# Modulation rows summed by halves, with additions made by accumulating DMAs, in a one-core hybrid decoder block

## The chip, the cores and the metric

The kernel runs on one core of a Trainium2 chip. The core has five engines that each work through their own queue in order: TensorE (PE, with its weight loads shown apart as PEld), VectorE (DVE), ScalarE (ACT), GpSimd (POOL) and SyncE (SP). Transfers are issued from the queues of SP, ACT and POOL and run on 16 shared DMA engines. The metric is the device time of one execution in microseconds (us); lower is better. A profiled execution's span runs from its first to its last instruction on the engines, and its own time is a little longer.

## What is computed

The reference is one layer of a decoder trunk on x (1 x 512 x 1024, float32), conditioned by a vector c of 1024 numbers. The layer has two sub-layers, and each is wrapped in normalisation and in shift, scale and gate rows that come from c:

```python
mod = jax.nn.silu(c) @ mod_w + mod_b
shift1, scale1, gate1, shift2, scale2, gate2 = [m[:, None, :] for m in jnp.split(mod, N_MOD, axis=-1)]

h = rms_norm(x, g_pre_mix) * (1 + scale1) + shift1
(sc_b, sc_c, sc_x, q, k, v, z, xbc, dt_raw,
 gl_a, gl_b, gl_c) = split_columns(h @ w_in)
y_a = short_conv_mixer(sc_b, sc_c, sc_x, sc_conv_w) @ w_sc_out
y_b = stick_breaking_attention(q, k, v) @ w_sb_out
y_c = mamba2_mixer(z, xbc, dt_raw, ...) @ w_ssm_out
merged = (jax.nn.sigmoid(gl_a) * y_a + jax.nn.sigmoid(gl_b) * y_b
          + jax.nn.sigmoid(gl_c) * y_c)
x = x + gate1 * rms_norm(merged @ w_o, g_post_mix)

h2 = rms_norm(x, g_pre_ffn) * (1 + scale2) + shift2
gt, up = jnp.split(h2 @ w_ffn_in, 2, axis=-1)
x = x + gate2 * rms_norm((silu(gt) * up) @ w_ffn_out, g_post_ffn)
```

`mod_w` is 1024 x 6144: six parts of 1024 columns, one each for shift1, scale1, gate1, shift2, scale2 and gate2. What the change touches is the sum over the 1024 rows of `mod_w` for parts 2 to 5, the addition of `mod_b`, and the sum of the three gated branches in `merged`.

## The kernel before

Every large product is made exact to nearly float32 by splitting each operand into a rounded high part and a low rest: `split` (L146) copies the high part on ACT and subtracts it on DVE, and `mm3` (L150) multiplies high by high, high by low and low by high. Activations are kept with channels on the 128 partitions and the 512 tokens along the columns, so a typical matmul is 128 x 128 by 128 x 512, and a product over 1024 channels is 24 matmuls.

**Weights.** SP loads weights in chunks of up to 1 MB into a ring of three buffers (`raw_tile`, L74). `chunks` (L163) is the list of them in order of use; `load_chunk` (L175) issues the next. A weight chunk is split into pieces of 128 x 1024; `piece` (L212) hands out the next piece and sees to it that two further ones are already split (`LOOK` = 3); four buffers hold the split pieces. Chunks of kind "mod" are raw rows of `mod_w`; they stay unsplit, and `mod_chunk` (L221) hands them out.

**The start** (L316 to L399) has an order written out by hand. Here `start_mod` (L250) forms the sums for shift1 and scale1, 128 columns of each at a time, and `start_col` (L260) turns them into columns. The result tile of a step, `out_` (L256), lies in the small pool `sm`.

**Behind the start** the order on each engine is set by a planner. It takes the program's order as priority, estimates when each instruction's inputs will be there, and lets an engine that would stand idle take a later instruction that is ready. Attention's softplus steps are marked as high priority. What it decides is then fixed: on the chip each engine runs its queue in that order.

**The mixers.** `attention` (L560), `ssd` (L673) and `mods_in_turn` (L894) are generators that run beside the projections: each call of `pump` (L835) lets every one of them emit its next step. `gate` (L881) projects one 128-channel tile of a branch gate (24 matmuls into a tile `pgt`), pumps once, and takes the sigmoid. Six gates are formed first (L888); then a loop over `mp` = 0 to 3 (L936) forms six further gates and handles two tiles m of 128 merged channels. For each, three branch products `pb` are multiplied by their gate tile on DVE (L954); the second and third are added to the running sum on DVE (L956); the sum `acc` is split into `mh[m]` and `ml[m]` (L958 to L960). Tiles of 128 x 512 that live for a short time come from one pool of 41 (`t2`, L67).

**The modulation rows** of parts 2, 3 and 4 (gate1, shift2, scale2) are made in `mods_in_turn` during those gates, by quarters of 256 columns. For a quarter, `sums` (L896) loads 256 numbers of `mod_b` from POOL's queue (L903). It then forms the sum of eight products with `mod_acc` (L228): partition p of the chunk holds rows 8p to 8p+7 of `mod_w`, each is multiplied by silu(c) for that row and added, all on DVE. The bias row is added into partition 0 on DVE (L906) and the result is split (L908). One or two pumps later, `row` (L911) sums over the partitions with two matmuls by a matrix of ones. This leaves the row on all partitions, and DVE or ACT takes it out of PSUM into `G1`, `SH` or `SC` (L917 to L921). Part 5 (gate2) is made in the same way during the first half of the last product (L1088).

**The output projection** (L1012 to L1027) takes two blocks of 128 tokens at a time. For each of the first five of eight row steps k it multiplies `mh[k]`, `ml[k]` by a piece of `w_o`, 12 matmuls for both blocks; the last three steps are done block by block, so that the chain behind the first block (`x1_chain`, L975) starts early. Ahead of it POOL issues four loads of x (L967 to L968) into the buffer that the third branch used. The feed-forward part (from L1030) follows.

Of the kernel before, what the change touches and what calls it, by code (L numbers as in the profile page):

```python
# [13 lines left out]
P = 128  # L14
# [18 lines left out]
def hybrid_block(ctx: ExitStack, tc, x, c, mod_w, mod_b, g_pre_mix, g_post_mix, g_pre_ffn,  # L33
# [193 lines left out]

    def mod_acc(acc, mw):  # L228

        vec.tensor_scalar(acc, mw[:, 0], sc8[:, 0:1], None, op0=ALU.mult)  # L230
        for r in range(1, KD):
            vec.scalar_tensor_tensor(acc, mw[:, r], sc8[:, r:r + 1], acc, op0=ALU.mult,  # L232
                                     op1=ALU.add)


# [216 lines left out]

    def w_mod(part, q4):
        n0 = part * D + q4 * 256
        chunks.append(("mod", [[(0, KD, mod_w[:, n0:n0 + 256])]], 256, 0))
# [5 lines left out]
    mods = [(p_, q4) for p_ in (2, 3, 4) for q4 in range(4)]  # L461
    w_cols(w_in, C_XBC + 384, P)
# [20 lines left out]
    for hf in range(2):  # L483
        for k0 in range(0, MF, 4):
            w_rows(w_ffn_out, k0, min(4, MF - k0), half(hf), 512)
            if hf == 0 and k0 // 4 < 4:
                w_mod(5, k0 // 4)
    n_pieces = sum(ch[3] * len(ch[1]) for ch in chunks)
# [405 lines left out]
    def mods_in_turn(steps, rest):  # L894

        def sums(part, q4):  # L896
            dsts, gain, plus = rows_of[part]
            n0 = part * D + q4 * 256
            if gain is not None and q4 % 2 == 0:
                nc.gpsimd.dma_start(dsts[q4 // 2],  # L900
                                    gain[0, q4 * 256:q4 * 256 + 512].partition_broadcast(P))
            brow = sm.tile([1, 256], F32, tag="brow", name="brow", bufs=2)
            nc.gpsimd.dma_start(brow, mod_b[n0:n0 + 256].unsqueeze(0))  # L903
            acc = sm.tile([P, 256], F32, tag="macc", name="macc2")
            mod_acc(acc, mod_chunk())
            vec.tensor_tensor(acc[0:1, :], acc[0:1, :], brow, ALU.add)  # L906
            am = sm.tile([P, 2, 256], FR, tag="mah", name="mah", bufs=1)
            split(am[:, 0, :], am[:, 1, :], acc)  # L908
            return am

        def row(part, q4, am):  # L911
            dsts, gain, plus = rows_of[part]
            dst = dsts[q4 // 2][:, (q4 % 2) * 256:(q4 % 2) * 256 + 256]
            pm = bank("pmr")
            pe.matmul(pm[:, 0:256], onesr, am[:, 0, :], start=True, stop=False)
            pe.matmul(pm[:, 0:256], onesr, am[:, 1, :], start=False, stop=True)
            if gain is None:  # L917
                act.copy(dst, pm[:, 0:256])
            else:
                vec.scalar_tensor_tensor(dst, pm[:, 0:256], plus, dst, op0=ALU.add,  # L920
                                         op1=ALU.mult)  # L921
        last = None
        for n, st_ in enumerate(steps):
            if last is not None:
                row(*last)
            last = st_ + (sums(*st_),)
            yield
            if rest and n % 2:
                yield
# [3 lines left out]

    mh, ml = [], []
    sides.append(mods_in_turn(mods, True))
    for mp in range(4):  # L936
# [6 lines left out]
        for j in range(2):  # L943
# [3 lines left out]
            for b, (k0, nk, bh, bl) in enumerate(((0, 2, yah, yal), (2, 2, ybh, ybl),  # L947
# [7 lines left out]
                if b:  # L955
                    vec.tensor_tensor(gt, gt, acc, ALU.add)  # L956
# [55 lines left out]
    for tp2 in range(2):  # L1012
# [63 lines left out]
    for hf in range(2):  # L1076
# [5 lines left out]
        for i in range(NPF - LATE):  # L1082
# [3 lines left out]
            if hf == 0:  # L1086
                if i == 0:
                    sides.append(mods_in_turn([(5, q4) for q4 in range(4)], False))  # L1088
                pump()
# [59 lines left out]
```

## Time and profile before

| | us |
|---|---|
| median of 3 runs | 808.54 |
| lowest and highest | 807.54, 809.47 |
| profiled execution, its own time | 807.41 |
| span of the profiled execution | 805.7 |
| mean granted TensorE clock in it | 0.997 of full speed |

The profile names instructions by line and by tile: L232 is line 232, `macc` the modulation sum, `wraw` a chunk of weights, `whi` and `wlo` a split piece. An arrow reads "written from". "Idle before <- releaser" tells how long an engine stood idle ahead of an instruction, and what ended that. On a page or in a view, busy time of PE counts matmuls that overlap, since each lasts longer than the distance to the next one.

### The profile page before, as it was taken

How to read it: one execution, taken by the hardware profiler on the slowest of the kernel's cores; microseconds unless marked ns; L12 is line 12 of the kernel's file. 1: busy time of each engine (PE TensorE's matmuls, PEld its weight loads, DVE VectorE, ACT ScalarE, POOL GpSimd, SP SyncE). 2: the span in 40 equal slices, each digit the busy share in tenths (PEclk: the TensorE clock that was granted, in tenths of full speed). 3: DMA queues.
4: the chain of work that ended last, by engine and by line, in shares of the span. 5: the costliest groups of instructions: out<-in, count | busy, mean ns of one | idle time of the engine just before them, and what ended most of it. 6: DMA issues, size and time to landing. Idle time of an engine off the chain costs nothing.

```text
span 805.7 us, 9651 instructions
## 1 busy us (share of the span) xinstructions
PE 775.2 (96%) x3677; PEld 634.2 (79%) x3677; DVE 495.5 (62%) x783; ACT 373.2 (46%) x625; POOL 122.5 (15%) x169
## 2 busy tenths in 40 slices
PE   3899999999899999999999999999999999999997
PEld 2679887767578888888878988888888888888886
DVE  5999968568967968748498544334344357423214
ACT  5566544565667445463465534434334433213112
POOL 4453412345421000000033000000000000000000
PEclk9999999999999999999999999999999999999999
DMA  9981441120534566452754322322333345532102
GB/s 281 297 258 58 130 131 53 53 85 31 184 121 154 187 201 206 129 173 101 262 169 145 102 84 78 103 81 79 102 105 104 105 148 195 170 115 96 35 1 105
DMA packets 96959, 105.07 MB, mean 130 GB/s; under 512 B 3276, under 2 KB 86272, under 8 KB 96912
## 3 DMA queue, kind: packets, MB, share of 16 engines
q1 hardware_dynamic: 94320, 99.62, 38.6%
q0 software_dynamic: 1824, 3.75, 1.6%
q10 hardware_dynamic: 768, 1.07, 0.4%
q8 instruction: 29, 0.48, 0.2%
q14 instruction: 18, 0.15, 0.1%
HBM read 102.33 MB, written 2.10 MB: 130 GB/s over the span
## 4 chain that ended last, share of the span: by engine, by line
PE 83%; DVE 11%; DMA 2%; issue 2%; ACT 1%; POOL 1%; DVEq 0%; POOLq 0%
PE pgt L151 5%; PE pgt L153 5%; PE pgt L152 5%; PE pfg L152 5%; PE pfu L152 5%; PE pfu L151 5%; PE pfg L151 5%; PE pfu L153 4%; PE pfg L153 4%; PE pfo L152 4%; PE pfo L153 4%; PE pfo L151 4%; DVE smacc L254 2%; PE pbr L151 2%; PE pbr L152 2%; PE pbr L153 2%
## 5 line engine op out<-in xcount | busy, mean ns | idle before, releaser
L147 ACT CAST whi<-wraw 128x1024 fp32r<-128x1024 f32 (+1 forms) x133 | 137.7, 1035 | 303.4 <-PE pfg L152 77.5
L148 DVE TENSOR_TENSOR wlo<-wraw,whi 128x1024 fp32r<-128x1024 f32 (+1 forms) x133 | 164.4, 1236 | 152.8 <-ACT whi L147 148.0
L151 PE MATMUL pgt<-hh,whi 128*128 128x512 f32 x192 | 75.7, 394 | 0.0
L153 PE MATMUL pgt<-hh,wlo 128*128 128x512 f32 x192 | 75.4, 393 | 0.0
L152 PE MATMUL pgt<-hl,whi 128*128 128x512 f32 x192 | 75.4, 393 | 0.0
L152 PE MATMUL pfu<-h2l,whi 128*128 128x512 f32 x160 | 63.0, 394 | 0.0
L152 PE MATMUL pfg<-h2l,whi 128*128 128x512 f32 x160 | 63.0, 394 | 0.0
L151 PE MATMUL pfu<-h2h,whi 128*128 128x512 f32 x160 | 62.7, 392 | 0.0
L151 PE MATMUL pfg<-h2h,whi 128*128 128x512 f32 x160 | 62.7, 392 | 0.0
L153 PE MATMUL pfu<-h2h,wlo 128*128 128x512 f32 x160 | 62.1, 388 | 0.0
L153 PE MATMUL pfg<-h2h,wlo 128*128 128x512 f32 x160 | 62.1, 388 | 0.0
L153 PE MATMUL pfo<-whi,fl 128*128 128x512 f32 x154 | 60.9, 395 | 0.0
L152 PE MATMUL pfo<-wlo,fh 128*128 128x512 f32 x154 | 60.9, 395 | 0.0
L151 PE MATMUL pfo<-whi,fh 128*128 128x512 f32 x154 | 60.8, 395 | 0.0
L903 POOL DMA_DIRECT2D brow<-in_mod_b_dram x16 | 8.1, 504 | 332.0 <-DVE macc L906 331.4
L232 DVE SCALAR_TENSOR_TENSOR macc<-wraw,sc,macc 128x256 f32<-128x256 f32 x112 | 55.8, 499 | 3.2
L153 PEld LDWEIGHTS pgt<-hh,wlo 128*128 128x128 f32 x192 | 36.1, 188 | 8.2
L151 PEld LDWEIGHTS pgt<-hh,whi 128*128 128x128 f32 x192 | 36.1, 188 | 7.8 <-issue 0.4
L152 PEld LDWEIGHTS pgt<-hl,whi 128*128 128x128 f32 x192 | 36.1, 188 | 7.5
L1061 DVE TENSOR_TENSOR f<-f,pfu 128x512 f32<-128x512 f32 x20 | 13.8, 688 | 40.3 <-PE pfu L153 40.3
L151 PEld LDWEIGHTS pfu<-h2h,whi 128*128 128x128 f32 x160 | 30.0, 188 | 7.0
L151 PEld LDWEIGHTS pfg<-h2h,whi 128*128 128x128 f32 x160 | 30.0, 188 | 7.0
(360 smaller groups left out, 1701.5 us busy)
## 6 DMA issues: line engine op xcount, KB each, us to landing
wraw<-in_w_ffn_in_dram SPq DMA_DIRECT2D x22, 1024.0 KB, 5.1
wraw<-in_w_in_dram SPq DMA_DIRECT2D x20, 1024.0 KB, 5.3
wraw<-in_mod_w_dram SPq DMA_DIRECT2D x16, 1024.0 KB, 5.4
wraw<-in_w_ffn_out_dram SPq DMA_DIRECT2D x10, 1024.0 KB, 5.0
wraw<-in_mod_w_dram SPq DMA_DIRECT2D x16, 512.0 KB, 6.1
wraw<-in_w_o_dram SPq DMA_DIRECT2D x8, 1024.0 KB, 4.9
xn<-in_x_dram SPq DMA_DIRECT2D x8, 256.0 KB, 5.7
wraw<-in_w_ssm_out_dram SPq DMA_DIRECT2D x4, 512.0 KB, 7.0
```

Of the source, the lines that this page charges most:

```text
L147: act.copy(hi, src)
L148: vec.tensor_tensor(lo, src, hi.bitcast(F32), ALU.subtract)
L151: pe.matmul(o, whi, xhi, start=start, stop=False)
L152: pe.matmul(o, whi, xlo, start=False, stop=False)
L153: pe.matmul(o, wlo, xhi, start=False, stop=stop)
L232: vec.scalar_tensor_tensor(acc, mw[:, r], sc8[:, r:r + 1], acc, op0=ALU.mult, op1=ALU.add)
L254: vec.scalar_tensor_tensor(acc[:, r % 2, :], mw2[:, r], sc8[:, r:r + 1], acc[:, r % 2, :], op0=ALU.mult, op1=ALU.add)
L903: nc.gpsimd.dma_start(brow, mod_b[n0:n0 + 256].unsqueeze(0))
L1061: vec.tensor_tensor(f, f, pu, ALU.mult)
```

## The change

- A "mod" chunk now holds four of the eight rows of each partition, 512 columns wide, in place of eight rows of 256 columns. Its size stays 1 MB, and the number of chunks 16.
- `mods_in_turn` works by halves of a part: two chunks make one half. The first of the eight products is taken on ACT, the other seven on DVE, all 512 columns wide. The sum lies in one buffer. `mod_acc` is gone.
- The bias row is added by a DMA from POOL's queue that accumulates from DRAM into partition 0 of the sum; the split comes one pump later. `row` runs once per half, 512 columns wide, between the two chunks of the next half.
- The second and third gated branch are added to the first by DMAs from POOL's queue that accumulate from one tile of the chip's memory into another, 128 x 512 each, in place of two DVE additions per tile.
- A merged tile is split after the next tile's products, the last one after the second row step of the output projection.
- The result tile of `start_mod` moves from the small pool to the pool `t2`.

```diff
-                pat = "(p k) n -> p k n" if kind == "mod" else "(k p) n -> p k n"
-                nc.sync.dma_start(raw[:, k0:k0 + nk, :], src.rearrange(pat, k=nk))
+                src = src if kind == "mod" else src.rearrange("(k p) n -> p k n", k=nk)
+                nc.sync.dma_start(raw[:, k0:k0 + nk, :], src)
...
-        out_ = sm.tile([P, 256], F32, tag="macc", name="macc")
+        out_ = t2("macc")[:, 0:256]
...
+    def w_mod(part, hf, rh):
+        n0 = part * D + hf * 512
+        src = mod_w[:, n0:n0 + 512].rearrange("(p r) n -> p r n", r=KD)
+        chunks.append(("mod", [[(0, 4, src[:, 4 * rh:4 * rh + 4, :])]], 512, 0))
...
+        def row(part, hf, am):
             dsts, gain, plus = rows_of[part]
+            dst = dsts[hf]
+            pm = bank("pmr")
+            pe.matmul(pm, onesr, am[:, 0, :], start=True, stop=False)
+            pe.matmul(pm, onesr, am[:, 1, :], start=False, stop=True)
+            if gain is None:
+                act.copy(dst, pm)
+            else:
+                vec.scalar_tensor_tensor(dst, pm, plus, dst, op0=ALU.add, op1=ALU.mult)
+        last = None
+        for part, hf in steps:
+            n0 = part * D + hf * 512
+            gain = rows_of[part][1]
+            if gain is not None:
+                nc.gpsimd.dma_start(rows_of[part][0][hf],
+                                    gain[0, hf * 512:hf * 512 + 512].partition_broadcast(P))
+            acc = sm.tile([P, 512], F32, tag="macc2", name="macc2", bufs=1)
+            for rh in range(2):
+                mw = mod_chunk()
+                for r in range(4):
+                    c_ = sc8[:, 4 * rh + r:4 * rh + r + 1]
+                    if rh + r == 0:
+                        act.activation(acc, mw[:, r], AF.Copy, scale=c_)
+                    else:
+                        vec.scalar_tensor_tensor(acc, mw[:, r], c_, acc, op0=ALU.mult,
+                                                 op1=ALU.add)
+                if rh == 0:
+                    yield
+                    if last is not None:
+                        row(*last)
+            nc.gpsimd.dma_start(acc[0:1, :], mod_b[n0:n0 + 512].unsqueeze(0), accum_op=ALU.add)
+            yield
+            am = sm.tile([P, 2, 512], FR, tag="mah", name="mah", bufs=1)
             split(am[:, 0, :], am[:, 1, :], acc)
+            last = (part, hf, am)
+            if rest:
                 yield
         yield
         row(*last)
...
+    def split_merged():
+        mh.append(t2("mh", FR))
+        ml.append(t2("ml", FR))
+        split(mh[-1], ml[-1], merged.pop(0))
...
                 vec.tensor_tensor(gt, gt, pb, ALU.mult)
                 if b:
-                    vec.tensor_tensor(gt, gt, acc, ALU.add)
-                acc = gt
-            mh.append(t2("mh", FR))
-            ml.append(t2("ml", FR))
-            split(mh[m], ml[m], acc)
+                    nc.gpsimd.dma_start(acc, gt, accum_op=ALU.add)
+                else:
+                    acc = gt
+            if merged:
+                split_merged()
+            merged.append(acc)
...
                 wo_mm(pos[tb], tb, ws[k], k)
+            if merged and k == 1:
+                split_merged()
```

More of the change, by code (lines that the diff above doesn't have):

```diff
@@ L226, in mod_chunk @@
         return raws[i]
[L228 to L233, printed above, removed]
     V = cp.tile([P, 72], F32, name="V")
@@ L460, in w_proj @@
                                  (4, 4, w_ssm_out[:, cs])]], 256, 2))
-    mods = [(p_, q4) for p_ in (2, 3, 4) for q4 in range(4)]
+    mods = [(p_, hf, rh) for p_ in (2, 3, 4) for hf in range(2) for rh in range(2)]
     w_cols(w_in, C_XBC + 384, P)
@@ L486, in hybrid_block @@
             if hf == 0 and k0 // 4 < 4:
-                w_mod(5, k0 // 4)
+                w_mod(5, k0 // 8, k0 // 4 % 2)
     n_pieces = sum(ch[3] * len(ch[1]) for ch in chunks)
@@ L894, in mods_in_turn @@
     def mods_in_turn(steps, rest):
-        def sums(part, q4):
+        def row(part, hf, am):
             dsts, gain, plus = rows_of[part]
[L898 to L907, printed above, removed]
-            split(am[:, 0, :], am[:, 1, :], acc)
-            return am
@@ L911, in row @@
[L911 to L928, printed above, removed]
+            dst = dsts[hf]
[6 more added lines that the diff above has]
+                vec.scalar_tensor_tensor(dst, pm, plus, dst, op0=ALU.add, op1=ALU.mult)
@@ L931, in mods_in_turn @@
         row(*last)
-    mh, ml = [], []
-    sides.append(mods_in_turn(mods, True))
+    mh, ml, merged = [], [], []
+    def split_merged():
+        mh.append(t2("mh", FR))
+        ml.append(t2("ml", FR))
+        split(mh[-1], ml[-1], merged.pop(0))
+    sides.append(mods_in_turn([(p_, hf) for p_ in (2, 3, 4) for hf in range(2)], True))
     for mp in range(4):
@@ L1087, in hybrid_block @@
                 if i == 0:
-                    sides.append(mods_in_turn([(5, q4) for q4 in range(4)], False))
+                    sides.append(mods_in_turn([(5, hf) for hf in range(2)], False))
                 pump()
```

3 lines of the change are left out of this document (removed).

## The prediction

> **What bounds the kernel now.** I read the page first, then busy time by stretches, then the chain of waits inside the one stretch where TensorE runs dry.
>
> ```profile
> span 805.7 us, 9651 instructions
> PE 775.2 (96%) x3677; PEld 634.2 (79%) x3677; DVE 495.5 (62%) x783; ACT 373.2 (46%) x625; POOL 122.5 (15%) x169
> PE 83%; DVE 11%; DMA 2%; issue 2%; ACT 1%; POOL 1%; DVEq 0%; POOLq 0%
> ```
>
> TensorE is busy 96% of the span and makes 83% of the chain that ended last. So an instruction saved on DVE or ACT is worth nothing where TensorE already runs without a gap. The stretches say where it does not:
>
> ```profile
> 0.00:60.00 60.00, 42.89 (x198) 34.09 (x199) 48.81 (x108) 33.95 (x75) 29.18 (x47) 1.00 0.98 278
> 160.00:200.00 40.00, 38.17 (x200) 29.71 (x199) 28.71 (x58) 25.55 (x49) 20.40 (x24) 1.00 0.17 53
> 200.00:245.00 45.00, 41.88 (x195) 30.77 (x194) 35.71 (x60) 28.01 (x50) 16.40 (x20) 0.96 0.44 144
> 245.00:384.00 139.00, 139.00 (x615) 113.94 (x616) 106.04 (x178) 69.97 (x106) 7.67 (x15) 1.00 0.53 168
> 400.00:425.00 25.00, 23.94 (x109) 18.72 (x109) 22.48 (x28) 16.20 (x34) 7.93 (x4) 1.00 0.50 166
> 425.00:445.00 20.00, 18.56 (x135) 16.88 (x133) 16.76 (x23) 11.67 (x31) 6.96 (x4) 1.00 0.35 109
> 445.00:660.00 215.00, 215.00 (x985) 178.36 (x985) 92.23 (x108) 90.23 (x121) 0.00 (x0) 1.00 0.30 97
> ```
>
> The columns are the stretch, its length, busy time of PE, PEld, DVE, ACT and POOL, the granted clock, DMA share and GB/s. TensorE misses 17.1 us in the start, which the edit leaves alone but for the home of one tile, 1.8 us in 160 to 200, 3.1 us in 200 to 245, and 2.5 us in 400 to 445. It is full from 245 to 384, where nearly all the edited work lies, and in 445 to 660. So the edit can win only in 160 to 245, and can lose anywhere. The 3.1 us are one hole:
>
> ```profile
> 208.49 0.71 ACT L590 ACTIVATE sb_e<-sb_e,one_c 128x512 f32<-128x512 f32 x1
> ...
> 206.74 1.12 DVE L230 TENSOR_SCALAR macc<-wraw,sc 128x256 f32<-128x256 f32 x1
> 207.89 3.21 DVE L232 SCALAR_TENSOR_TENSOR macc<-wraw,sc,macc 128x256 f32<-128x256 f32 x5
> 211.02 0.68 DVE L591 SCALAR_TENSOR_TENSOR sb_e<-pz,sb_e 128x512 f32<-128x512 f32 x1
> ...
> 210.54 0.40 PE L153 MATMUL pgt<-hh,wlo 128*128 128x512 f32 x1
> 212.83 0.50 PE L625 MATMUL pz<-sb_hi,negtri 128*128 128x512 f32 x1 [1.89 <-DVE sb_hi L596]
> 214.56 0.80 PE L625 MATMUL pz<-sb_lo,negtri 128*128 128x512 f32 x1 [1.23 <-DVE sb_lo L597]
> ...
> 215.99 2.36 PE py L790 x16
> 218.78 0.43 PE pb L764
> 219.21 0.23 PE pgt L151
> 225.73 1.30 PE py L790 x16
> 227.03 0.43 PE py L794 x4
> ```
>
> ACT hands over attention's last tile at 208.49 + 0.71 = 209.20. DVE takes it up (L591) only at 211.02, 1.82 us late, because six operations of the second modulation sum stand ahead of it in its queue. TensorE then waits 1.89 us for `sb_hi` and 1.23 us for `sb_lo`, and the 16 `py` matmuls behind the hole take 2.36 us where the next such 16 take 1.30: 1.06 us of slower clock. The earlier gaps, 1.8 us in 160 to 200, left the granted clock at 1.00.
>
> **The change part by part.** Durations, one row for each kind:
>
> ```profile
> L232 DVE SCALAR_TENSOR_TENSOR macc<-wraw,sc,macc 128x256 f32<-128x256 f32 x112 | 55.8, 499 | 3.2
> L956 DVE TENSOR_TENSOR gate<-gate 128x512 f32<-128x512 f32 x16 | 11.1, 691 | 0.5
> L906 DVE TENSOR_TENSOR macc<-macc,brow 1x256 f32<-1x256 f32 x16 | 8.1, 505 | 0.3
> L148 DVE TENSOR_TENSOR mah<-macc,mah 128x256 fp32r<-128x256 f32 x16 | 6.6, 415 | 0.0
> L230 DVE TENSOR_SCALAR macc<-wraw,sc 128x256 f32<-128x256 f32 x16 | 6.4, 399 | 4.5 <-DMA wraw<-in_mod_w_dram 4.3
> L148 DVE TENSOR_TENSOR ml<-gate,mh 128x512 fp32r<-128x512 f32 x8 | 5.5, 685 | 0.0
> L865 DVE SCALAR_TENSOR_TENSOR cc<-up,V,cc 128x512 f32<-128x512 f32 x4 | 3.0, 746 | 0.0
> L159 ACT ACTIVATE gate<-gate 128x512 f32<-128x512 f32 x24 | 15.1, 631 | 0.6
> ```
>
> *Sums by halves.* Two quarters of 256 columns cost DVE 2 x (0.399 + 7 x 0.499 + 0.505 + 0.415) = 9.6 us. One half of 512 costs 7 x 0.746 + 0.685 = 5.9 us, 746 ns being the same operation at 512 columns (L865). Eight halves give DVE 30 us back. ACT gets eight first products (631 ns for the nearest 512-wide form, 5.0 us in all), some of it returned by splitting once per half. TensorE has 16 row matmuls of 512 columns for 32 of 256: the same columns, nothing. The loads are the same 16 x 1 MB.
>
> *What that is worth in the hole.* Two 4-operation groups now make a half. The second group needs the second chunk, as the six operations did. If it stands where they stood, it takes 4 x 0.746 = 2.98 us from 206.74. L230 took 1.12 us there against 0.399 on average, an extra 0.72 us; with that delay carried over L591 starts at 210.4, without it at 209.7, and if the group has run before, at 209.2. So L591 is 0.6, 1.3 or 1.8 us earlier. I take the middle, 1.3, off the 1.89 us wait. The wait for `sb_lo` stays, since a weight split stands in front of it. What is left, 3.1 - 1.3 = 1.8 us, is a gap like the one that cost no clock, so the 1.06 us of slow `py` go too. Term: 1.3 + 1.06 = **2.4 us**. Upper end: the whole hole. From 210.77 (the last gate matmul's start, 210.54, plus the 0.23 us from matmul to matmul) to 218.78 TensorE does four `pz` matmuls of 512 and 384 columns, 0.8 us at that pace, and `py` work that takes 1.30 + 0.43 us in the next group, so 8.0 - 2.5 = 5.5 us. Lower end: the planner's new order puts a wide operation ahead of another attention step and makes a second hole like this, -5.5 us.
>
> *Bias row by DMA.* It takes 0.505 us off DVE, and puts a landing between the last product and the split. The split is one pump later, so the planner has a gate of about 5.5 us (24 matmuls, 0.23 us apart) to fill.
>
> ```profile
> L903 POOL DMA_DIRECT2D brow<-in_mod_b_dram x16: 484/494/561, 3.1 to 672.3; - x16
> DMA to landing us min/median/max: 1.8/5.1/6.4
> ...
> 216.03 0.60 ACT L629 ACTIVATE sb_at<-pz 128x512 f32<-128x512 f32 x1 [3.70 <-PE pz L625]
> ```
>
> Landing is 1.8 to 6.4 us for the same row now. The instruction that waits is ACT's copy; behind it are the sigmoids and weight casts. Cover: TensorE has up to three pieces split ahead, each a gate long, so at 6.4 us it costs nothing outside attention. Inside it, ACT idles 3.70 us before 216.03, and a short landing fits there. I take 0; the range is from a loss of 2.7 us (6.4 less 3.7) to 0.
>
> *Merge by DMA.* It takes 16 x 0.691 = 11.1 us off DVE in 265 to 384, where TensorE is full: nothing by itself. No accumulating DMA is in this trace. The nearest are POOL's 256 KB row loads and its 512 KB loads of x:
>
> ```profile
> L900 POOL DMA_DIRECT2D G<-in_g_post_mix_dram x2: 543/562/582, 243.0 to 243.6; - x2
> DMA to landing us min/median/max: 3.4/3.6/7.4
> ...
> L968 POOL DMA_DIRECT2D x<-in_x_dram x4: 528/532/557, 381.7 to 383.3; - x4
> DMA to landing us min/median/max: 4.0/5.2/8.9
> ...
> 379.28 0.68 DVE L954 TENSOR_TENSOR gate<-gate,pbr 128x512 f32<-128x512 f32 x1
> ...
> L151 PE MATMUL pwo<-whi,mh x64: 393/394/483, 380.9 to 428.5; 128*128 128x512 f32 x64
> ...
> 383.98 1.05 ACT L147 CAST whi<-wraw 128x1024 fp32r<-128x1024 f32 x1 [0.77 <-PE pwo L153]
> ```
>
> The two merges of a tile follow each other: the second adds to what the first wrote, so it waits for the landing, on POOL, which has nothing else to do there but the x loads. For the last tile: product ready at 379.28 + 0.68 = 379.96, then twice 0.55 of issue and a landing. At 3.6 us (same size, so my value) the tile is whole at 388.3; at 1.8, 384.7; at 8.9, 398.9. Who waits is ACT's split and, behind it, the casts of the output projection's weights. A row step there is 12 matmuls, 2.8 us, from 380.9. If the split stands ahead of the cast now at 383.98, that piece (fifth step, needed at 380.9 + 4 x 2.8 = 392.1) needs 0.62 + 1.05 + 1.23 us behind the landing, which must be at 389.2 or before. At 388.3 there is 0.9 us to spare: 0, and up to 9.7 us lost at the far end. All earlier tiles have a whole tile's 5.5 us and more. POOL gets 16 issues and loses 8: 4.4 us on an engine 15% busy. Behind a merge that waits there stand the gain and bias rows, which the pumps need a gate later, and at the end the x loads: behind the second merge they go out at 384.7, 3.0 us later than now, and even 8.9 us of landing ends at 393.6 for the first, before the first block's last row step at 397.7. Cost 0.
>
> A rule of the Trainium skill speaks for a shorter landing: "DMA: Bandwidth & Descriptors", section "Anatomy of one DMA — SWDGE (gpsimd) path", gives about 2.0 us plus bytes over 436 GB/s, an estimated 2.6 us for 256 KB. By it the tile is whole at 386.3, and the sum is the same; the trace's 3.6 us for that size is longer, and a load from HBM.
>
> *Split one later, tile's home.* Same operations; the last split, after the second of eight row steps, is used from 380.9 + 14.0 + 2.8 = 397.7. Nothing. The 2.5 us in 400 to 445 (x1 chain against weight splits) is untouched.
>
> **Sum.** -2.4 us on the profiled execution's 807.41 (span 805.7 and 1.7 around it) is 805.0. That execution lies 1.1 under the median of 808.54; in terms of the median, **806.1**.
>
> **Rivals.** (a) *The hole stays.* The four wide operations still stand ahead of L591, or the next half's first group, whose chunk may come earlier now that chunk buffers are freed sooner, takes their place: 0.6 us at most, 807.9 to 808.5. For it: DVE's order is the planner's, and it fills with sums whatever idle time it expects. Against it: 30 us of such filling is gone. This is also the case where 41 us less DVE work does nothing, DVE not being the bound. (b) *Late merge.* Landings of 6.1 us each make the last tile whole at 379.96 + 2 x 6.65 = 393.3, 4.1 us past 389.2; with the 2.4 won that is 810.2, and 815.8 at 8.9 us. It decides from about 6 us a landing. For it: the four x loads, 2 MB, can stand ahead of the second merge in POOL's queue, and landed in up to 8.9 us. Against: median 3.6 at this size. "SBUF — State Buffer", section "SBUF: two separate sides", in the Trainium skill warns that a DMA issued by GpSimd waits for its descriptors while DVE runs a two-port copy (about 0.62 us alone, 3.1 beside one); by that estimate a landing of 3.6 becomes 6.1 and this rival the result. The trace shows issues of 0.48 to 0.58 us on POOL and nothing stretched to 3. (c) *A second hole* in attention, from the new order or the bias landing: 2.4 won, 5.5 lost, 811.6.
>
> **Chances.** The forecast, hole shrunk or gone (803.0 to 806.9): 0.46. (a): 0.32. (b): 0.14. (c): 0.08. About 0.2%, 1.6 us, is what a measurement of this kernel can tell from no change. Faster 0.46, same 0.32, slower 0.22. The forecast's own range is 803.0 to 806.9; the range of 8 in 10 goes on over (a) and the near part of (b) and (c): 803.0 to 811.0.
>
> **What would show it.** Right: 200 to 245 has TensorE at 43.5 us or more, its clock near 1.00, no wait of L625 on `sb_hi` over 0.6 us; 245 to 400 still full; the span shorter by what that stretch gains. (a): the same L625 wait with a sum operation ahead of L591. (b): ACT waiting for a DMA between 384 and 392, and TensorE idle just after. (c): a new wait of `pz` or `po` matmuls between 110 and 245. Wrong altogether: the gain lies in the start, in 400 to 445 or in the tail.

## The result, and the profile after

The changed kernel takes 813.33 us in the median of six runs (812.05 to 815.96). The kernel before, measured with it, took 809.0 in the median of six. The ratio on record, which is estimated from all these runs and not from the two medians, is 1.0063, with a 95% interval of 1.0037 to 1.0089: 0.6% slower, where 806.1 us had been forecast. In the experiments below, two executions that were far slower than all others of the same kernel are left out, one of best_x (860.05 us) and one of the kernel before (1557.49 us). The profiled execution took 814.04 us. From its page:

```profile
span 812.3 us, 9545 instructions
...
PE 776.9 (96%) x3661; PEld 633.9 (78%) x3661; DVE 458.4 (56%) x665; ACT 376.1 (46%) x623; POOL 135.0 (17%) x177
...
PE 45%; DVE 4%; DMA 2%; issue 1%; ACT 1%; DVEq 0%; POOL 0%; ACTq 0%; POOLq 0%
```

DVE has lost 37 us of work (495.5 to 458.4), as the change intended, and TensorE is still busy for 96% of the span. (The shares of the chain add up to about half only, because the view follows it no further back than 376 us.) The busy time of stretches (columns as in the prediction) tells where the 6.6 us of longer span lie. First the kernel after, then the one stretch of before that the prediction did not show:

```profile
0.00:60.00 60.00, 41.54 (x190) 32.35 (x191) 44.47 (x103) 33.23 (x71) 23.45 (x43) 1.00 0.95 274
160.00:200.00 40.00, 38.17 (x200) 29.72 (x199) 28.68 (x59) 24.76 (x48) 18.43 (x24) 1.00 0.22 68
200.00:245.00 45.00, 42.27 (x202) 31.54 (x201) 36.03 (x50) 29.66 (x53) 20.53 (x19) 1.00 0.46 150
245.00:384.00 139.00, 139.00 (x608) 113.60 (x607) 76.93 (x97) 68.89 (x100) 18.33 (x23) 1.00 0.63 186
384.00:400.00 16.00, 12.56 (x51) 9.60 (x50) 6.48 (x7) 6.34 (x8) 2.50 (x4) 0.94 0.81 235
400.00:425.00 25.00, 24.99 (x102) 19.63 (x100) 18.82 (x25) 15.03 (x32) 6.71 (x4) 0.90 0.60 207
```

```profile
384.00:400.00 16.00, 16.00 (x70) 12.92 (x69) 6.42 (x6) 6.58 (x9) 0.00 (x0) 1.00 0.84 313
```

In 384 to 400 TensorE was full and now lacks 3.4 us; behind that its clock is 0.94 and 0.90 of full speed. In 400 to 425 it looks busier than before (24.99 against 23.94), but it does fewer matmuls (102 against 109): they are slower. The start lacks 1.4 us more. In 200 to 245 TensorE misses 2.7 us where it missed 3.1, and the clock there is 1.00 in place of 0.96.

Marks on TensorE say it more exactly, since each is the first matmul of a part of the program. The tile views of the kernel after, with the count, the durations and then the first and last start:

```profile
L151 PE MATMUL pq<-hh,whi x16: 391/394/394, 80.5 to 90.8; 128*128 128x512 f32 x16
...
L151 PE MATMUL pgt<-hh,whi x192: 388/394/502, 182.9 to 357.8; 128*128 128x512 f32 x192
...
L151 PE MATMUL pwo<-whi,mh x64: 392/394/628, 380.9 to 435.1; 128*128 128x512 f32 x64
...
L151 PE MATMUL pf<-h2h,whi x64: 278/280/393, 435.8 to 462.2; 128*128 128x256 f32 x64
```

The same marks of before are 78.0 for `pq`, 180.3 to 357.8 for `pgt`, 380.9 for `pwo`, and 429.2 for `pf`. So the loss falls into three terms:

| | before | after | |
|---|---|---|---|
| start, up to the first `pq` | 78.0 | 80.5 | +2.5 |
| first `pq` to last `pgt` (attention and gates) | 279.8 | 277.3 | -2.5 |
| last `pgt` to first `pwo` | 23.1 | 23.1 | 0.0 |
| first `pwo` to first `pf` (output projection) | 48.3 | 54.9 | +6.6 |
| sum, at the first `pf` | 429.2 | 435.8 | +6.6 |

**The hole in attention** shrank. The timeline of the kernel after (its lines stand five lower: L586 is the old L591, L591 the old L596, L620 the old L625):

```profile
209.32 2.93 DVE L917 SCALAR_TENSOR_TENSOR macc<-wraw,sc,macc 128x512 f32<-128x512 f32 x2
...
210.40 0.72 ACT L585 ACTIVATE sb_e<-sb_e,one_c 128x512 f32<-128x512 f32 x1
...
212.17 0.68 DVE L586 SCALAR_TENSOR_TENSOR sb_e<-pz,sb_e 128x512 f32<-128x512 f32 x1
...
214.31 0.50 PE L620 MATMUL pz<-sb_hi,negtri 128*128 128x512 f32 x1 [1.39 <-DVE sb_hi L591]
...
215.04 0.50 PE L620 MATMUL pz<-sb_lo,negtri 128*128 128x512 f32 x1 [0.22 <-DVE sb_lo L592]
```

Two of the new wide products, not four, stand ahead of attention's step. ACT is done at 210.40 + 0.72 = 211.12 and DVE takes the tile up at 212.17, 1.05 us late in place of 1.82. TensorE waits 1.39 + 0.22 us where it waited 1.89 + 1.23, and the clock no longer drops behind the hole: before, it was 0.50 of full speed from 214.4 to 217.8. From the last gate matmul ahead of the hole to the first behind it TensorE takes 5.53 us (212.53 to 218.06) where it took 8.51 (210.54 to 219.05), 3.0 us less.

**The bias row** takes 2.0 us of that back, in the next group of `py` matmuls. `dec` is a factor that DVE, ACT and POOL form in turn for `py`:

```profile
217.68 0.62 ACT L147 CAST mah<-macc 128x512 fp32r<-128x512 f32 x1 [5.80 <-DMA macc<-in_mod_b_dram]
...
222.52 1.38 DVE L768 TENSOR_SCALAR dec<-pb,acs 128x256 f32<-128x256 f32 x4
...
225.75 0.87 PE L785 MATMUL py<-dec,xdt 128*64 128x256 f32 x8 [0.58 <-POOL dec L771]
227.15 0.65 PE L785 MATMUL py<-dec,xdt 128*64 128x256 f32 x4 [0.54 <-POOL dec L771]
```

ACT stands for 5.80 us at the landing of the bias row. The cast of a weight piece behind it comes late, DVE waits for that cast (2.67 us, until 219.28), and so DVE starts `dec` 4.8 us after the `pb` matmul at 217.71 that it needs; before, it started 1.0 us after it (219.67 and 218.71). TensorE then waits 0.58 + 0.54 us for POOL. From the `po` matmuls to the next gate it takes 4.72 us (223.66 to 228.38) where it took 2.74 (224.66 to 227.40).

**The last merge** is the loss. The chain of waits of the kernel after, from 376 to 412 us (start, length, what):

```profile
376.15 0.86 DMA gate<-gate
377.01 4.62 issue
...
382.18 5.06 DMA gate<-gate
...
387.77 8.38 DMA gate<-gate
...
399.05 0.80 PE pwo L152
399.85 0.43 PE pwo L153
...
404.54 0.43 PE pwo L152
```

POOL issues the merges one after the other, and the second of a tile only behind the landing of its first. Tile 6's second merge goes out at 381.64, the first of tile 7 right behind it (382.18 in the chain); that one lands 5.06 us later, and the second of tile 7, issued at 387.77, takes 8.38 us. The timeline of the same stretch shows who stands behind it:

```profile
382.71 1.24 POOL L974 DMA_DIRECT2D x<-in_x_dram  x1
...
387.77 0.86 POOL L961 DMA_DIRECT2D gate<-gate  x1 [3.82 <-DMA gate<-gate]
...
388.33 1.94 POOL L974 DMA_DIRECT2D x<-in_x_dram  x3
...
394.71 0.40 PE L153 MATMUL pwo<-whi,ml 128*128 128x512 f32 x1
396.18 0.62 ACT L147 CAST mh<-gate 128x512 fp32r<-128x512 f32 x1 [8.66 <-DMA gate<-gate]
396.70 3.88 ACT L147 CAST whi<-wraw 128x1024 fp32r<-128x1024 f32 x4
...
397.79 0.51 PE L151 MATMUL pwo<-whi,mh 128*128 128x512 f32 x1 [2.69 <-ACT whi L147]
```

ACT stands for 8.66 us at the split of the last tile, with four casts of `w_o` queued behind it. TensorE uses up the pieces that were ready until 394.71, then waits 2.69 us for a cast and 0.75 us for the rest of that split: 3.4 us. Twelve matmuls after that (399.85 to 404.54 in the chain) stand 0.43 us apart in place of 0.23, another 2.4 us, and the slow first one adds 0.6: together 6.4 of the 6.6 us. The granted clock in this stretch, 398.15 to 404.97, is 0.50.

**The start** orders its loads otherwise. SP's timeline before, then after:

```profile
14.76 5.99 SPq L80 DMA_DIRECT2D wraw<-in_mod_w_dram  x4
20.79 1.83 SPq L89 DMA_DIRECT2D wxr<-in_w_in_dram  x1
```

```profile
14.36 7.83 SPq L80 DMA_DIRECT2D wraw<-in_mod_w_dram  x5
22.24 1.84 SPq L89 DMA_DIRECT2D wxr<-in_w_in_dram  x1
```

Five loads of `mod_w` now stand where four stood, and the next weights of the first projection (`wxr`) are issued 1.5 us later. The waits of the first 70 us have ACT waiting 9.6 us for `wxr` in nine waits, where it was 1.1 us in three.

### The profile page after: what moved, and what is told of

Read it like the earlier page. It is cut to its first block, busy times and chain, and to the rows that moved or that the text cites. A ratio compares the mean times of both kernels' runs of the same rounds, so it can differ in the third digit from the quotient of the medians.

```text
span 812.3 us, 9545 instructions
## 1 busy us (share of the span) xinstructions
PE 776.9 (96%) x3661; PEld 633.9 (78%) x3661; DVE 458.4 (56%) x665; ACT 376.1 (46%) x623; POOL 135.0 (17%) x177
## 4 chain that ended last, share of the span: by engine, by line
PE 45%; DVE 4%; DMA 2%; issue 1%; ACT 1%; DVEq 0%; POOL 0%; ACTq 0%; POOLq 0%
PE pfg L151 5%; PE pfu L151 5%; PE pfu L153 5%; PE pfg L153 5%; PE pfg L152 4%; PE pfu L152 4%; PE pfo L153 4%; PE pfo L152 4%; PE pfo L151 4%; DMA gate<-gate 2%; DVE wlo L148 1%; DVE t2k L992 1%; DVE x L994 1%; DVE st L999 1%; PE pf L151 0%
## 5 line engine op out<-in xcount | busy, mean ns | idle before, releaser
L148 DVE TENSOR_TENSOR wlo<-wraw,whi 128x1024 fp32r<-128x1024 f32 (+1 forms) x133 | 162.0, 1223 | 160.9 <-ACT whi L147 160.7
L923 POOL DMA_DIRECT2D macc<-in_mod_b_dram x8 | 6.8, 850 | 281.5 <-DVE macc L917 236.8
L917 DVE SCALAR_TENSOR_TENSOR macc<-wraw,sc,macc 128x512 f32<-128x512 f32 x56 | 45.4, 812 | 9.2 <-ACT macc L915 4.2
L153 PEld LDWEIGHTS pfu<-h2h,wlo 128*128 128x128 f32 x160 | 30.0, 188 | 7.0
L153 PEld LDWEIGHTS pfg<-h2h,wlo 128*128 128x128 f32 x160 | 30.0, 188 | 7.0
L152 PEld LDWEIGHTS pfu<-h2l,whi 128*128 128x128 f32 x160 | 30.0, 188 | 6.7
```

Of the source, the lines that this page charges most:

```text
L148: vec.tensor_tensor(lo, src, hi.bitcast(F32), ALU.subtract)
L152: pe.matmul(o, whi, xlo, start=False, stop=False)
L153: pe.matmul(o, wlo, xhi, start=False, stop=stop)
L917: vec.scalar_tensor_tensor(acc, mw[:, r], c_, acc, op0=ALU.mult, op1=ALU.add)
L923: nc.gpsimd.dma_start(acc[0:1, :], mod_b[n0:n0 + 512].unsqueeze(0), accum_op=ALU.add)
```

## The experiments

Two theories stood for the output projection: the merge's late landing holds the casts (rival (b) of the prediction), or the last split itself comes too late for TensorE. For the start: the one tile whose home moved, or the new loads later on. All kernels below compute the whole reference. The three sets ran beside 29, 33 and 19 runs of the kernel before, with medians of 807.18, 807.23 and 807.47 us. The table has the ratios on record and the marks from each profiled execution, one for each kernel; the text then takes the kernels in turn.

| | ratio to before, interval | up to `pq` | `pq` to last `pgt` | `pwo` to `pf` |
|---|---|---|---|---|
| before | | 78.0 | 279.8 | 48.3 |
| after | 1.0063 [1.0037, 1.0089] | 80.5 | 277.3 | 54.9 |
| last_dve | 1.0001 [0.9991, 1.0010] | 80.5 | 278.3 | 48.2 |
| casts_first | 1.0002 [0.9990, 1.0013] | 80.6 | 277.4 | 48.3 |
| x_later | 1.0003 [0.9994, 1.0012] | 79.8 | 278.0 | 48.3 |
| merge_only | 1.0063 [1.0047, 1.0080] | 78.3 | 282.8 | 54.4 |
| out_home | 1.0051 [1.0037, 1.0064] | 77.7 | 277.3 | 56.1 |
| start_only | 1.0035 [1.0021, 1.0048] | 80.5 | 280.1 | 48.3 |
| best_last | 0.9987 [0.9976, 0.9999] | 78.9 | 277.8 | 49.3 |
| best_x | 0.9990 [0.9977, 1.0004] | 77.3 | 277.1 | 48.3 |
| best_bias | 0.9997 [0.9984, 1.0010] | 77.2 | 277.9 | 49.0 |
| best_merge | 0.9973 [0.9964, 0.9983] | 77.9 | 277.4 | 48.2 |
| best_six | 0.9968 [0.9956, 0.9981] | 79.6 | 277.8 | 48.2 |

**The eighth tile added on DVE** (last_dve), the other seven by DMA:

```diff
+                    if m >= 7:
+                        vec.tensor_tensor(acc, acc, gt, ALU.add)
+                    else:
-                    nc.gpsimd.dma_start(acc, gt, accum_op=ALU.add)
+                        nc.gpsimd.dma_start(acc, gt, accum_op=ALU.add)
```

> Edit: only the last merged tile (m = 7) is added on DVE again; the other seven tiles keep their accumulating DMAs. Theory (late last merge: the last tile's second merge lands at 396 us, ACT's split waits for it, the casts of the output projection's weights stand behind it, TensorE runs dry at 394.9): the wait goes, TensorE is full from 384 to 400, the output projection ends about 6 us earlier, 806 to 808 us against 813.3. Rival (4 MB of merge traffic slows the weight loads, so that seven of eight merges leave the loss): at least 5 of the 6.6 us stay, 811 or more. Rival (the 2.5 us that the start got longer are the whole loss): 813.

The output projection is back at 48.2 us and the whole loss of the median is gone: 807.26 us. Two DVE additions, of the kind that took 0.69 us each before, were worth 5 us by the two ratios (1.0063 and 1.0001) and 6.7 by the mark. What is left is the start's loss and attention's gain, which nearly cancel (+2.5 and -1.5 by the marks).

**The last split behind the casts** (casts_first). The merges stay DMAs; a one-column copy ties the last split to the eighth weight piece, so that it can't stand ahead of any cast:

```diff
+        if behind is not None:
+            act.copy(mh[-1][:, 0:1], behind[:, 0, 0:1].bitcast(F32))
...
-            if merged and k == 1:
-                split_merged()
...
+        if merged:
+            split_merged(ws[KD - 1][0])
```

> Edit: all merges stay DMAs; the split of the last tile is put behind the cast of the eighth weight piece on ACT's queue by a one-column copy from that piece into the split's destination. The landing is as late as before. Theory (it is the casts queued behind the waiting split that starve TensorE, not the tile itself): the tile is split by about 397.5 us, first used at 397.7, so TensorE waits under 1 us and the time falls to 807 to 809. Rival (TensorE waits for the tile itself): the hole stays, 812 to 814.

From its timeline:

```profile
392.54 1.05 ACT L147 CAST whi<-wraw 128x1024 fp32r<-128x1024 f32 x1 [1.75 <-PE pwo L153]
393.62 0.19 ACT L940 CAST mh<-whi 128x1 fp32r<-128x1 f32 x1
396.19 0.62 ACT L147 CAST mh<-gate 128x512 fp32r<-128x512 f32 x1 [2.39 <-DMA gate<-gate]
```

The tile lands as late as in the changed kernel (ACT splits it at 396.19, there at 396.18), and yet TensorE loses nothing:

```profile
384.00:400.00 16.00, 16.00 (x70) 12.84 (x69) 9.06 (x9) 8.48 (x12) 2.49 (x4) 1.00 0.92 283
```

The median is 807.80 us, as the theory had it. So it was not the tile that came too late for its own matmuls. It was the casts of other weights that stood behind it in ACT's queue.

**The x loads held back** (x_later), by one-column copies on POOL that wait for the last merge:

```diff
     for tb in range(NTB):
+        pool.tensor_copy(x1[:, tb, 0:1], merged[0][:, 0:1])
+    for tb in range(NTB):
         nc.gpsimd.dma_start(x1[:, tb, :], x[blk(tb), :])
```

> Edit: the four loads of x on POOL's queue are held back until the last merged tile is whole, by a one-column copy from that tile ahead of each. Theory (the loads of x, 1.5 MB queued just behind the last merge and 0.5 MB ahead of it, stretch its landing from about 4.2 us to 8.4): it lands in 4 to 5 us, at 391 to 392, and 3 to 4.5 us of the hole go: 808.5 to 810.5, if the loads of x are still in time for 408. Rival (the merge is slow by itself, or by the weight loads): the landing stays over 7 us and the time at 813.

```profile
387.10 0.86 POOL L961 DMA_DIRECT2D gate<-gate  x1 [3.79 <-DVE gate L959]
391.30 0.54 POOL L974 COPY x<-gate 128x1 f32<-128x1 f32 x4 [3.34 <-DMA gate<-gate]
391.91 2.15 POOL L976 DMA_DIRECT2D x<-in_x_dram  x4
```

Issued at 387.10, the last merge has landed by 391.2: some 4.1 us in place of 8.4, with SP's loads of `w_o` beside it as in the changed kernel (next issue at 387.97 and 388.10). So half of that landing was the 2 MB of x in POOL's own queue. The median is 807.34 us, better than the 808.5 to 810.5 expected: at a landing of 4.1 us nothing of the hole is left. TensorE is full in 384 to 400, and nobody misses the x that comes 3.6 us later (from 388.33 to 391.91).

**The merge alone** (merge_only): the kernel before with the merge by DMA and the late splits, its sums, bias and start unchanged.

```diff
-                    vec.tensor_tensor(gt, gt, acc, ALU.add)
-                acc = gt
+                    nc.gpsimd.dma_start(acc, gt, accum_op=ALU.add)
+                else:
+                    acc = gt
...
+            if merged and k == 1:
+                split_merged()
```

> The kernel before with the merge alone: the second gated branch added by the accumulating DMA, each tile split one later, the eighth behind two weight pieces of the output projection; the modulation rows and the start are those of before. The theory (the last tile's landing of 7 to 9 us holds the split, and the weights' casts queued behind it, whatever was gained before it): the stretch from pgt's first matmul to its last stays at 177.5 us, TensorE stands idle 3 to 5 us between 384 and 400, the ratio 1.005 to 1.009. The rival (the merge comes late only because the attention before it had become 2.6 us shorter and the rows' bias DMAs share POOL's queue): idle under 1.5 us there and a ratio under 1.003.

The waits of TensorE in this kernel, 245 to 425 us (total, times, longest):

```profile
PE pwo L151 <- ACT whi L147: 2.3, 1, 2.3
PE pmr L916 <- DVE mah L148: 2.0, 2, 1.1
PE pwo L152 <- DVE wlo L148: 0.5, 1, 0.5
```

The output projection loses 6.1 us and the ratio is 1.0063. Its idle time there is 2.8 us (2.3 + 0.5), of which 1.8 fall into 384 to 400, less than the 3 to 5 expected there; the rest is slow clock again: 0.86 in 400 to 425, and 0.50 from 400.5 to 407.3. (This execution was the slowest of the six, 816.56 us; their median is 812.77.) So the merge loses by itself; the other edits neither cause it nor need to be there. This kernel has a wait of 2.0 us for `mah` as well, in the gates, which neither before nor after has, and its gates take 178.7 us where 177.5 were expected.

**The start's tile back in the small pool** (out_home):

```diff
-        out_ = t2("macc")[:, 0:256]
+        out_ = outs[:, k % 2 * 256:k % 2 * 256 + 256]
```

> Edit: the result tile of the start's sums lies in the small pool again (in the two halves of the tile that the row sums use later), all else as in the changed kernel. Theory (the eight further tiles of the pool of 41 reorder the start's loads on SyncE and delay them, 2.5 us by the end of the start): the first projection behind the start begins 2 to 2.5 us earlier; what becomes of it by 380 us depends on attention's hole: 810.5 to 812.5. Rival (the 2.5 us are run to run): 813, the start as in the changed kernel.

SP has its old order again (four loads of `mod_w`, then `wxr` at 20.87), and `pq` starts at 77.7 us, 2.8 earlier than in the changed kernel. The ratio gains only 0.12% on it (1.0051 against 1.0063), about 1 us: the output projection, reached earlier by TensorE while the last merge goes out no earlier (388.17 against 387.77), is 1.2 us longer still, 56.1.

**The start's tile alone** (start_only): one line of the kernel before.

```diff
-        out_ = sm.tile([P, 256], F32, tag="macc", name="macc")
+        out_ = t2("macc")[:, 0:256]
```

> The kernel before with one line changed: the eight sums of the start (out_) take a tile of the 41-tile pool. The theory (the shifted rotation of that pool makes the planner order the start's loads otherwise, whatever becomes of the later parts): the first matmul of the convolution's weights (pq) moves from 78.0 to between 79.5 and 81, all later marks by as much, the span from 805.7 to 807.5 to 808.5 us, the ratio 1.002 to 1.004. The rival (the start is late in the changed kernel only because its later loads, in halves, are ordered otherwise): pq at 78.0 and a ratio within 0.001 of 1.

```profile
14.78 7.77 SPq L80 DMA_DIRECT2D wraw<-in_mod_w_dram  x5
22.60 1.84 SPq L89 DMA_DIRECT2D wxr<-in_w_in_dram  x1
```

The same five loads, `pq` at 80.5, the ratio 1.0035: the theory holds, and this one line costs 2.8 us. What in the planner's estimate tips the order was not pursued; that the tile's home does it is shown. The size is less sharp than the two marks suggest: `pq` starts at 79.8 to 80.6 in the five profiled executions with five loads ahead, and at 77.2 to 79.6 in the eight with four.

**Both losses mended** (best_last, best_x, best_bias). best_last has out_home's start and last_dve's merge; best_x has out_home's start and x_later's loads, all merges by DMA; best_bias is best_last with the bias loaded ahead and added on DVE, in two pieces:

```diff
-            nc.gpsimd.dma_start(acc[0:1, :], mod_b[n0:n0 + 512].unsqueeze(0), accum_op=ALU.add)
+            for j in range(2):
+                cell = (slice(32 * j, 32 * j + 1), slice(256 * j, 256 * j + 256))
+                vec.tensor_tensor(acc[cell], acc[cell], brow[cell[0], :], ALU.add)
```

> Edit: both repairs together, the start's result tile back in the small pool and the last merged tile added on DVE. Theory (the three effects are separate and add up: start +2.5, attention's hole -2.6, last merge +6.6): only the gain of the hole is left, 2.3 to 3 us under the kernel before, ratio 0.9965 to 0.9975; the output projection begins at about 378. Rival (the 2.6 us of the hole are the slack of a late start, made good whatever the sums cost): the same as before, ratio 1.000.

> Edit: the start's result tile back in the small pool, and the loads of x held behind the last merge; all 16 merges stay DMAs. Theory: as the run with the last tile on DVE, ratio 0.9965 to 0.998; merges by DMA cost nothing where nobody waits. Rival (held-back loads of x come late once the projection starts 2.7 us earlier): TensorE waits between 400 and 425 by 1 us more, ratio 0.999.

> Edit: as the run with both repairs, and the bias row is loaded ahead and added on DVE again, in two operations, in place of the accumulating DMA. Theory (the landing of the bias row lies under TensorE's work, as predicted): within 0.7 us of that run, and DVE gains two operations per half. Rival (ACT's wait for the bias row holds up attention): 1 us or more faster than that run, the waits of pz and py matmuls between 205 and 220 gone.

best_last gives 0.9987. By its parts it should have been near 0.9966: last_dve's 1.0001 less the 0.0035 of the start. Its trace has a short wait left:

```profile
389.48 0.50 PE L152 MATMUL pwo<-wlo,mh 128*128 128x512 f32 x1 [0.79 <-DVE wlo L148]
```

ACT splits tile 6, still merged by DMA, at 385.62, after 6.77 us of waiting, and the casts are late again. best_x has no wait in the output projection, and its profiled execution, span 802.3 us, is the shortest of the thirteen; but its timed runs go up to a span of 806.9, and by their median of 807.09 and a ratio of 0.9990, which is the rival's number, it can't be told from before. The rival's sign, a further wait between 400 and 425, is not in the trace; why the other runs are slower than the profiled one stays open. best_bias brings a wait back into attention:

```profile
PE pz L621 <- DVE sb_hi L592: 2.5, 1, 2.5
```

Two more small operations stand on DVE between the wide products and attention's step, and the clock in 200 to 245 is 0.96 again. On the other side the wait of `py` for `dec` is gone: from the `po` matmuls to the next gate TensorE takes 2.74 us (222.88 to 225.62), as before. The start of the gates' matmuls shows the same in all kernels: the nine with the bias by DMA need 1.6 to 2.0 us more there than the kernel before, and best_bias, start_only and merge_only nothing. But best_bias wins only 0.3 us in the hole where those nine win 3.0 to 3.8. In sum the bias by DMA is 0.5 to 0.8 us better by the marks (277.9 against 277.1 to 277.4 in the five kernels that have it and a clock of 1.00 in 160 to 200); the timed intervals of best_bias and best_last overlap, so that runs don't decide it.

**All merges on DVE** (best_merge: out_home's start, no merge by DMA; the halves, the bias by DMA and the later splits stay) and **the last two tiles on DVE** (best_six: as best_last, with `m >= 6`):

> Edit: the start's result tile back in the small pool, and all merges on DVE as in the kernel before: what is left of the change is the sums by halves with the bias row by DMA, and the later split. Theory: ratio 0.9965 to 0.9975, no different from the run where seven of eight tiles are merged by DMA, since 11 us of DVE time in 265 to 384 are worth nothing beside a full TensorE. Rival (the merges by DMA free DVE for something that counts): slower than that run by 1 us or more.

> The changed kernel with the start's tile in its old place and the last two merges (tiles 6 and 7) added on DVE, the other six by DMA. The theory (only the last two tiles have a deadline that a DMA of 5 to 8 us misses): TensorE idle under 0.5 us between 384 and 400, no wait of pwo for wlo, and a ratio of 0.9965 to 0.998, as with all eight merges on DVE (0.9973). The rival (the six DMAs left cost something elsewhere, by POOL's time or by the x loads behind them): 0.9985 to 1.000, as with the last tile alone on DVE (0.9987).

best_merge takes 804.87 us and best_six 804.69: ratios of 0.9973 and 0.9968, 2.2 and 2.6 us faster than before. Between the two nothing can be told. Both are faster than best_last (0.9987), which best_merge had been expected to equal: tile 6 had to leave the DMAs as well. TensorE in best_six:

```profile
384.00:400.00 16.00, 16.00 (x71) 12.82 (x70) 9.22 (x11) 7.13 (x11) 0.00 (x0) 1.00 0.81 293
```

So six merges by DMA cost nothing, and the 8 us of DVE work that they save win nothing either. Both kernels beat the two that were compared, by what attention and the gates gain.

The parts add up. The start alone is worth +0.35%, the merge alone +0.63%, and the sums (best_merge) -0.27%: together +0.71%, where the whole change measures +0.63%, within 0.37 to 0.89.

## Why the prediction was wrong, point by point

- **What bounds the kernel**: right. TensorE does, and 37 us less of DVE work is worth 2.2 to 2.6 us at most (best_merge, best_six).
- **The hole, -2.4 us**: right in place, a little small in size, and by another order than assumed. The hole gave 3.0 us: 1.5 of idle time, where 1.3 was forecast, and 1.5 of clock, where 1.06 was, because the slow spell had held the `pz` matmuls too and not only `py`. Not four wide products but two stand ahead of attention's step, and each takes 1.45 us, nearly twice the 0.746 that was assumed. Of the three signs that the prediction named for 200 to 245, only the clock of 1.00 came; TensorE is busy for 42.27 us in 200 to 245, not 43.5, and the wait for `sb_hi` is 1.39 us, not under 0.6.
- **The near match of -2.5 by the marks is luck.** By the starts of the gate matmuls it is made up of -0.6 ahead of the hole, which start_only and merge_only show as well and which is therefore not the sums' doing, -3.0 in the hole, +2.0 of the bias row, and -1.0 in small steps between 228 and 358, where TensorE waits for nothing in either kernel; the cause of these steps is open.
- **The bias by DMA, 0**: wrong by 2.0 us, inside the range of 0 to 2.7 given for it. It landed in 3.5 to 6.3 us, and ACT waited for it twice. The prediction let a short landing fit into ACT's idle time inside attention, but ACT stood until 217.68, and what was queued behind it came late for `dec` and so for TensorE. best_bias, without this DMA, does not have that loss.
- **The merge by DMA, 0**: this is the step that failed, in its landing of 3.6 us. The prediction had the last tile whole at 388.3 and the deadline at 389.2; it was whole at 396.15. Two terms were wrong. The first merge of tile 7 was taken to go out when its product was ready, at 379.96; it went out at 382.18, behind tile 6's second merge in POOL's queue (381.64), and landed at 387.24 in place of 384.1: 3.1 us. The second was given 0.55 of issue and 3.6 of landing and took 8.91: 4.8 us. Four loads of x lay around it, as rival (b) said for it; x_later shows that they are the cause of that half. "All earlier tiles have a whole tile's 5.5 us and more" left out that tile 6's own chain, from its first merge at 376.15 to its split at 385.00, reaches 5 us into tile 7's. It holds DVE too: the low part of tile 6's split stands there ahead of tile 7's third product, which ends only at 386.94, so that the second merge could not have gone out much sooner (in x_later, where the first lands at 386.40, this product is what releases it). The deadline was later than assumed: one more piece was cast ahead of the waiting split, TensorE ran on for five row steps, to 394.9, and by the prediction's own 2.9 us of split and cast the tile was needed at 392.0.
- **The landing by rule.** The Trainium skill, "DMA: Bandwidth & Descriptors", section "Anatomy of one DMA — SWDGE (gpsimd) path", gave an estimate of 2.6 us for the landing; the sixteen measured are 3.3 at the least, 4.2 in the median and 8.4 at most, so the rule lies under all of them. The other page of the Trainium skill, "SBUF — State Buffer", section "SBUF: two separate sides", spoke for a late merge. What stretched the landing here is the x loads; x_later mends it with DVE's work left as it is, so the wait for descriptors that this page tells of is not needed for it.
- **Rival (b)**: the right mechanism, with the casts behind the split as who waits, which casts_first shows. Its prices of 810.2 and 815.8, for landings of 6.1 and 8.9 us, enclose the profiled execution's 814.04; that they do is partly luck, since they hold neither the slow clock nor the start's loss. Its chance of 0.14 was too low. The rows quoted for it had x landings of up to 8.9 us in the same queue, and the margin was 0.9 us on two landings; a median of loads from another part of the program was taken for a transfer with 2 MB around it in its own queue.
- **"Split one later, tile's home. Nothing"**: wrong by 2.5 us (2.8 by the medians of start_only) for the home of the start's tile. The prediction looked at the operations, which are the same, and not at the order that the planner makes of them.
- **What was not priced**: the slow clock behind a new hole. Of the 6.6 us, 3.4 are idle time and 3.0 are matmuls at the slow clock.

The landing measures, from the views of the kernel after by line, for the issue's duration in ns and for the landing in us (min, median, max):

```profile
L961 POOL DMA_DIRECT2D gate<-gate x16: 860/883/1558, 273.1 to 387.8; - x16
...
DMA to landing us min/median/max: 3.3/4.2/8.4
```

## What to carry to other kernels

An addition made by DMA is cheap only where nobody waits for it: here six tiles of eight had the time, the last two had not, and what waited was not the tile's reader but everything queued behind its split. The bias row's landing is the same case in small: 5.80 us of ACT's queue, and 2 us of TensorE two engines further on. Before a dependent pair of transfers takes the place of two short operations, add up the whole queue that issues them, with the loads that share it, at the largest landing in the trace, not the median. And where a planner orders the program, a buffer's new home is a change of order: look for it at the far end of the kernel too.

## What the runs showed of the hardware

- An accumulating DMA of 256 KB from POOL's queue has an issue record of 0.86 us at the least, 0.88 in the median and 1.56 at most, where the loads of the kernel before had 0.48 to 0.58. The records overlap, though: two issues in a row go out 0.54 us apart (381.64 and 382.18), no further than loads. It lands after 3.3 to 8.4 us; with four 512 KB loads around it in the same queue the last one took 8.4, and with these held back 4.1.
- The 512-wide product with two inputs on DVE takes 0.73 to 0.75 us, but 1.45 on average in the pair at 209.32, most of which falls into POOL's work on two tiles (L771, 4.39 us from 207.32); no experiment took that work away; the largest of the 56 is 1.50.
- The same gap costs clock in one execution and not in the next. TensorE has a gap of about 1.8 us in 160 to 200 in all 13 profiled executions. In seven of them the clock there is 1.00 and the time from the first `pq` to the first `pgt` 102.3 to 102.5 us; in six it is 0.96 and 103.7 to 104.1. Kernels whose edits to the changed kernel concern only the last merge and what follows it stand on both sides (after and casts_first in the seven, last_dve and x_later in the six). So the "gap that cost no clock", from which the prediction argued, costs some 1.5 us in about half of the executions, and one profiled execution can't tell which. In the nine kernels with the wide sums and the bias by DMA only 0.4 to 1.2 us of it are left by the last `pgt`, as the hole in attention is shorter where the clock dropped ahead of it (TensorE waits 0.5 to 0.6 us for `sb_hi`, and not 1.4).
- Where the clock drops, it reads 0.50 over a short stretch: 180.5 to 183.9 in last_dve, 214.4 to 217.8 in the kernel before, 398.15 to 404.97 in the kernel after, that is 3.4, 3.4 and 6.8 us. The 3.4 us of waits in the kernel after thus cost 3.0 more in slow matmuls.
